# Summing a row-times-matrix product over 16 streamed weight blocks: on the tensor engine, or on the vector engine with a final sum over partitions

## The chip, the cores and the metric

The kernel runs on one core of a Trainium2 chip. The metric is the device time of one execution in microseconds (us). PE is the tensor engine (matmuls; PEld is its weight load), DVE the vector engine, ACT the scalar engine, POOL the GpSimd engine, SP the engine that issues most DMAs. Each engine works through its own instructions in the order in which the program gives them, and waits on semaphores for what others produce.

## What is computed

Two transformer blocks over 256 tokens of width 1024. The first block begins with a modulation: six rows of 1024 numbers, made from one conditioning vector `c`.

```python
sc = jax.nn.silu(c)
shift1, scale1, gate1, shift2, scale2, gate2 = jnp.split(sc @ w_mod + b_mod, 6, axis=-1)
h = modulate(rms_norm(x, norm1_g), shift1, scale1)
y, _ = token_mixer(h, hc, P, last)       # attention, gated linear attention (gla), hyena; merged by w_out
x = x + gate1[:, None, :] * y
h = modulate(rms_norm(x, norm2_g), shift2, scale2)
x = x + gate2[:, None, :] * grouped_moe(h, ...)
```

The change concerns the last four of the six rows (gate1, shift2, scale2, gate2), "the second modulation": a vector of 1024 times a matrix of 1024 x 4096, 16 MB of float32. The rows are first used where `w_out`'s result is evicted, so there is the whole token mixer to stream the matrix in.

## The kernel before

**Tiling.** `stream_order` (L249) lays all weights out as blocks of mostly 1 MB (128 partitions x 8 KB). `load` (L501) has SP fetch them in that order into buffers of the tag u8, of which there are 19 of 8 KB per partition (`BUFS`, L325); weight pieces, activations and other large tiles use the same 19. An ordinary weight piece is split by `stream` (L527) into a rounded high part (ACT) and the rest (DVE), and `feat_block` (L624) multiplies it: one half block is 24 matmuls of 256 columns. The second modulation's matrix comes as 16 blocks of [128, 2048] (`mod2`): blocks 0 to 7 are the eight chunks of the contraction for the first 2048 columns (the first half: gate1, shift2), blocks 8 to 15 for the other 2048 (scale2, gate2). They stand between the blocks of the three branches, by `MOD2_BRG` and `MOD2_BR` (L334): 0 to 3 beside the gate columns `w_brg` of the attention branch, 4 to 7 beside `w_br_att`, 8 to 11 beside `w_brg` of gla, 12 and 13 beside `w_br_gla`, 14 and 15 beside the first two blocks of `w_brg` of hyena.

**The product.** `mod_block` (L1353) multiplies one block when its place comes. `mod_rows` (L815) issues four matmuls, one for each 512 columns; the weights on the array are a column of `cs` (silu of `c`) padded to 32 columns, so the four results stand in partition groups 0, 32, 64 and 96 of one PSUM bank, held over eight blocks. After block 7 and after block 15 DVE adds the bias tile `bm` to it; `mod_spread` (L1389) then splits the sum into high and low part and copies each row to all 128 partitions by matmuls with `pick`, a matrix with ones in rows 0, 32, 64 and 96. `mod_spread` is a generator: for the first half one step of it is taken at the start of each of blocks 8 to 15, for the second half all steps are taken by `spread` (L1502) ahead of the last quarter of `w_out`.

**The order of the work around it.** The program is emitted in one sequence, and each engine keeps that order. Main work (weight blocks) is emitted in order; the chains of attention, gla and hyena are generators whose steps are put between the main work by a planner, `Side` (L383) with `Clocked` (L341). The planner keeps a clock for PE, ACT and DVE of its own: a matmul of n columns costs n/2400 us (4n/2400 if its operands are not rounded ones or n is under 256), a DVE operation 0.07 + n/960, an ACT operation 0.06 + n/1150. After each piece of main work `tick` looks whether a step is due:

```python
def tick(self):
    if self.jobs and Clocked.now["P"] >= self.next()[1]:
        self.step()
# step: wait = next(job); if wait: due = Clocked.now["P"] + wait
#       else: due = (last end of an ACT or DVE operation of the step) + 0.15
def finish(self, g):          # emits what is left of job g, step after step
    while any(j[0] is g for j in self.jobs):
        self.step(...)
```

Three lines of the main program call `finish` (L1428): attention must be complete before `w_br_att` starts, gla before `w_br_gla`, hyena before `w_br_hy`. Only one step goes at a tick. Attention's steps ask for a wait of 6.0; most of gla's and hyena's are due 0.15 after their last ACT or DVE operation. Between 160 and 455 us of the trace this sets the order. The `w_out` product follows (`lin_sq`, L1453, call at L1560), then the router and the experts.

Of the kernel before, what the change touches and what calls it, by code (L numbers as in the profile page):

```python
# [12 lines left out]
AF = mybir.ActivationFunctionType  # L13
OP = mybir.AluOpType
# [4 lines left out]
D = 1024  # L19
# [363 lines left out]
class Side:  # L383
# [10 lines left out]
    def next(self):  # L394

        a = self.jobs[:2]
        return a[1] if len(a) > 1 and a[1][2] is a[0][0] and a[1][1] < a[0][1] else a[0]
# [22 lines left out]
def program(ctx, tc, A, out, dump=None):  # L420
# [5 lines left out]
    V, S, G, P = nc.vector, nc.scalar, nc.gpsimd, nc.tensor  # L426
    V, S, P = Clocked(V, "V"), Clocked(S, "S"), Clocked(P, "P")
# [4 lines left out]
    def T(shape, name, dt=F32, tag=None):  # L432
        n = 4
        for s in shape[1:]:
            n *= s
        if tag is None:
            for t, lim in (("us", 128), ("uh", 512), ("u1", 1024), ("u2", 2048), ("u4", 4096), ("u8", 8192)):
                if n <= lim:
                    tag = t
                    break  # L440
        uid[0] += 1
        t = sb.tile(list(shape), dt, tag=tag, bufs=BUFS.get(tag, 1), name=f"{name}{uid[0]}")
        return t

    def T2(shape, name):

        n = 4 * math.prod(shape[1:])
        if n > 4096:
            return T(shape, name + "H", F32R), T(shape, name + "L", F32R)
        t = T([shape[0], 2, *shape[1:]], name, F32R)  # L450
        return t[:, 0], t[:, 1]

    def PS(name="ps"):
        uid[0] += 1
        t = pp.tile([128, 512], F32, tag="ps", bufs=8, name=f"{name}{uid[0]}")
        return t

    def mm3(ps, aH, aL, bH, bL, start, stop):
        P.matmul(ps, aH, bH, start=start, stop=False)
        P.matmul(ps, aH, bL, start=False, stop=False)  # L460
        P.matmul(ps, aL, bH, start=False, stop=stop)

    def split(h, l, src):
        S.activation(h, src, AF.Copy)
        V.tensor_tensor(l, src, h, op=OP.subtract)
# [86 lines left out]
    def take(name, b, u=0):  # L552
        i, v = pieces[pos["take"]]
        assert order[i][:2] == (name, b) and u == v, (order[i], v, name, b, u)
        stream()
        pos["take"] += 1
        return halves.pop((i, u)) if order[i][4] is not None else raws.pop(i)
# [66 lines left out]
    def feat_block(name, b, x, per=1):  # L624

        for u in range(2):
            wh, wl = take(name, b, u)
            for j in range(per):
                g = u * per + j
                if g % 2 == 0:  # L630
                    ps = PS()
                lin_feat(wh, wl, j, x, ps[:, (g % 2) * 256:(g % 2) * 256 + 256])
                side.tick()
                if g % 2:
                    yield ps
# [10 lines left out]
    def C(name):  # L646
        g, sl = CCOLS[name]
        return cg[g][:, sl]
# [21 lines left out]
    rows = {}  # L670
# [13 lines left out]
    pick = T([128, 128], "pick", F32R)  # L684
# [7 lines left out]
    st = {}  # L692
# [119 lines left out]
    cs = T([128, 8, 32], "cs", tag="cs")  # L812
    V.memset(cs, 0.0)

    def mod_rows(w, k, ps):  # L815
        for j in range(4):
            P.matmul(ps[32 * j:32 * j + 32], cs[:, k], w[:, 0, j * 512:j * 512 + 512], start=k == 0, stop=k == 7)
# [46 lines left out]
    mrow = T([128, 512], "mrow")  # L864
# [41 lines left out]
    def by_k(pair):  # L906
        return lambda k: (pair[0][:, k], pair[1][:, k])

    def xs_of(pair):
        def f(k, m):  # L910
            c = slice(m * 128, m * 128 + 128)
            return pair[0][:, k, c], pair[1][:, k, c]
        return f
# [158 lines left out]
    ps = PS()  # L1072
# [275 lines left out]
    hyj = side.add(hyj)  # L1348


    acc2, mod2, spreads = {}, [], []

    def mod_block(i):  # L1353

        hf, k = divmod(i, 8)
        w = take("mod2", i)
        if hf:
            next(spreads[0], None)
        if k == 0:
            acc2[hf] = PS("mod")  # L1360
        mod_rows(w, k, acc2[hf])
        if k == 4:
            st["bm"] = bm = T([128, 512], "bm", tag="u4")
            V.memset(bm, 0.0)
            for j in range(4):
                S.dma_start(bm[32 * j:32 * j + 1], A["b_mod2"][:, hf * 2048 + j * 512:hf * 2048 + j * 512 + 512])
        if k == 7:
            bm = st["bm"]
            V.tensor_tensor(bm, acc2.pop(hf), bm, op=OP.add)
            spreads.append(mod_spread(st.pop("bm")))  # L1370
            if False:
                next(spreads[hf])

    rw = Pc("router_w").rearrange("p (k e) -> p k e", k=8)

    def turned_half(src, k4):
        pt = PS()
        for k in range(4):
            P.transpose(pt[:, k * 128:k * 128 + 128], src[:, (4 * k4 + k) * 128:(4 * k4 + k) * 128 + 128], ident)
        t = T([128, 512], "h2T")  # L1380
        S.activation(t, pt, AF.Copy)
        return t

    def logits(ts, ps, start, stop):

        for k in range(8):
            P.matmul(ps, ts[k // 4][:, k % 4 * 128:k % 4 * 128 + 128], rw[:, k], start=start and k == 0, stop=stop and k == 7)

    def mod_spread(rows):  # L1389

        rH, rL = T2([128, 512], "mrow")
        split(rH, rL, rows)
        yield
        for a in range(2):
            t = T([128, D], "mod2")
            for n in range(2):
                ps = PS()
                q = slice(32 * (2 * a + n), 32 * (2 * a + n) + 32)
                P.matmul(ps, pick[q], rH[q], start=True, stop=False)
                P.matmul(ps, pick[q], rL[q], start=False, stop=True)  # L1400
                S.activation(t[:, n * 512:n * 512 + 512], ps, AF.Copy)
            mod2.append(t)
        yield
        if len(mod2) == 2:
            ts = [turned_half(mod2[1], k4) for k4 in range(2)]
            yield
            ps = PS()
            logits(ts, ps[:, :16], True, True)
            st["shifted"] = T([128, 16], "shifted", tag="uh")
            V.tensor_copy(st["shifted"], ps[:, :16])  # L1410

    msum = mH = mL = None
    n_mod = 0
    for b, br in ((2, "att"), (1, "gla"), (0, "hy")):
        g = T([128, 8, 256], "gate")
        for j in range(4):
            ps, = feat_block("w_brg", 4 * b + j, by_k(hs[0]))
# [13 lines left out]
        if br == "hy":  # L1431
            xt = T([128, 2, D], "x")
            G.dma_start(xt, A["x"].rearrange("(m p) d -> p m d", p=128))
            mH, mL = T2([128, 8, 256], "m")
        per = 2 if br == "att" else 4
        for i in range(8 // per):
            for j, ps in enumerate(feat_block("w_br_" + br, i, ys, per // 2)):
                c = slice(per * i + 2 * j, per * i + 2 * j + 2)
# [10 lines left out]
        if br == "att":  # L1449
            msum = g  # L1450
    dump("mH", mH)

    def lin_sq(name, xs, evac, before=(), quarters=(0, 1, 2, 3), whole=None):  # L1453


        ps = {(m, n): PS() for m in range(2) for n in range(2)}
        kept = []

        def go(m, n, q, w):
            for k in range(2):  # L1460
                first, last = q == quarters[0] and k == 0, q == quarters[3] and k == 1
                if whole and q in WHOLE:
                    P.matmul(ps[m, n], whole(2 * q + k, m), w[:, k, n * 512:n * 512 + 512], start=first, stop=last)
                else:
                    h, l = xs(2 * q + k, m)
                    mm3(ps[m, n], h, l, w[0][:, k], w[1][:, k], first, last)
            side.tick()

        for i, q in enumerate(quarters):
            if q in before:  # L1470
                before[q]()
            if i == 2 and "prepare" in st:
                st.pop("prepare")()
            for n in range(2):
                if n == 0 or not (whole and q in WHOLE):
                    block = take(name, q, n)
                w = (n, q, block)
                go(0, *w)
                if i:
                    kept.append(w)  # L1480
                else:
                    go(1, *w)
                if i == 3:
                    evac(0, n, ps[0, n])
        for n in range(2):
            for w in kept:
                if w[0] == n:
                    go(1, *w)
            evac(1, n, ps[1, n])
# [67 lines left out]
        P.matmul(pa[m][n], ident, x1[:, m, n * 512:n * 512 + 512], start=True, stop=False)  # L1557

    psr = PS()
    lin_sq("w_out", xs_of((mH, mL)), ev_out, {3: spread}, whole=lambda k, m: msum[:, k, m * 128:m * 128 + 128])  # L1560
    for k4 in range(2):
        turned.append(turned_half(h2s[1][0], k4))
        if not k4:
# [25 lines left out]
    def ahead(v, count):  # L1589
# [21 lines left out]
                           op0=OP.is_lt, op1=OP.mult)  # L1611
# [4 lines left out]
    ps = PS()  # L1616
# [80 lines left out]
    with tc.If(full > CAP, label="full"):  # L1697
# [10 lines left out]
        for e in range(N_EXP):  # L1708
# [9 lines left out]
            for k in range(8):  # L1718
                for q in range(2):
                    w = fetch("gu", 8 * e + k, q)  # L1720
                    for m in range(2):
                        P.matmul(gu[q, m], fT[m][:, k * 128:k * 128 + 128], w, start=k == 0, stop=k == 7)
            for m in range(2):
                hf, ht, ps = hfs[m], hts[m], gu[0, m]
# [6 lines left out]
            for k in range(4):  # L1731
                for n in range(2):
                    w = fetch("down", 4 * e + k, n)
# [83 lines left out]
    for w, n in (("a", 8), ("b", 16)):  # L1817
# [4 lines left out]
        k = T([128, 2 * n], "rk", tag="us")  # L1822
# [26 lines left out]
    for e in range(N_EXP):  # L1849
# [3 lines left out]
        ps = PS()  # L1853
# [504 lines left out]
```

## Time and profile before

| | |
|---|---|
| median of 3 runs | 1425.87 us (1422.07 to 1426.35) |
| the profiled execution | 1420.13 us, of it a span of 1418.4 us from the first to the last instruction |
| PE, PEld busy | 96%, 75% of the span |
| DVE, ACT busy | 59%, 45% |
| mean granted clock of PE | 0.992 of 2.4 GHz |

An operation's duration in the profile overlaps with the next one's start on the same engine, so where many follow each other the distance of their starts is the price. A matmul in plain float32 shows as two records.

### The profile page before, as it was taken

The page shows a single profiled execution, that of the slowest core. Times are in us where ns is not written, and L with a number is a line of the kernel's source. Part 1 is how long each engine was busy: PE and PEld are TensorE (multiplying, and loading weights), DVE is VectorE, ACT ScalarE, POOL GpSimd, SP SyncE. Part 2 cuts the span into 40 slices and gives each one's busy share as a digit, 9 for nine tenths or more (in the row PEclk, how much of TensorE's full clock was granted, in tenths as well). Part 3 has the DMA queues.
Part 4 walks back from the last instruction along what each step waited for, and adds up shares of the span by engine and source line. Part 5 has one row for each costly group of instructions (what it writes and reads, how often), then busy time and mean ns, then how long its engine had stood idle before and what let it go on. Part 6 is the DMA issues. An engine that isn't in the chain of part 4 may idle for free.

```text
span 1418.4 us, 20472 instructions
## 1 busy us (share of the span) xinstructions
PE 1365.9 (96%) x8334; PEld 1065.1 (75%) x8334; DVE 836.1 (59%) x1519; ACT 634.6 (45%) x1020; POOL 5.8 (0%) x13
## 2 busy tenths in 40 slices
PE   6999999999999899999999899999999998999998
PEld 2678899878797444343488679999978887999996
DVE  5777457446766511211465586666676888566675
ACT  5544465544333311111357555544526673455541
POOL 0000000000000000000000000000000000000000
PEclk9999999999999999999999999999999999999999
DMA  9523344635469799999742345555444353555630
GB/s 373 219 71 119 149 151 154 247 130 196 161 210 360 307 421 420 421 420 421 275 179 89 119 145 182 208 178 208 165 162 149 127 179 135 191 179 178 215 142 30
DMA packets 44481, 297.42 MB, mean 210 GB/s; under 512 B 5170, under 2 KB 6370, under 8 KB 10016
## 3 DMA queue, kind: packets, MB, share of 16 engines
q1 hardware_dynamic: 41868, 291.02, 54.6%
q10 hardware_dynamic: 1924, 3.27, 0.7%
q0 software_dynamic: 592, 1.79, 0.5%
q8 instruction: 67, 1.10, 0.3%
q14 instruction: 30, 0.25, 0.0%
HBM read 295.00 MB, written 1.05 MB: 209 GB/s over the span
## 4 chain that ended last, share of the span: by engine, by line
PE 56%; DVE 5%; ACT 2%; DMA 1%; issue 1%; ACTq 0%; SPq 0%; DVEq 0%
PE ps L379 47%; PE pd L379 7%; DVE w L379 2%; PE pa L379 1%; PE pq L379 1%; ACT pe L379 1%; DVE v L379 1%; DMA raw<-in_ab_q 1%; DVE sm L379 1%; ACT w L379 0%; DVE rs L379 0%; PE oc L379 0%; DVE xL L379 0%; DVE rsa L379 0%; DMA pt<-in_p 0%
## 5 line engine op out<-in xcount | busy, mean ns | idle before, releaser
L379 DVE TENSOR_TENSOR w<-raw,w 128x1024 fp32r<-128x1024 f32 (+3 forms) x301 | 346.4, 1194 | 84.5 <-ACT w L379 83.4
L379 ACT ACTIVATE w<-raw 128x1024 fp32r<-128x1024 f32 (+3 forms) x301 | 293.5, 1033 | 10.8 <-DVE w L379 4.8
L379 PE MATMUL ps<-xH,w 128*128 128x256 f32 x1408 | 256.5, 283 | 0.6 <-ACT xH L379 0.6
L379 PEld LDWEIGHTS ps<-xH,w 128*128 128x128 f32 x1408 | 220.6, 192 | 1.8 <-ACT xH L379 1.1
L379 PE MATMUL ps<-xL,w 128*128 128x256 f32 x704 | 199.3, 283 | 0.7 <-DVE xL L379 0.7
L379 PE MATMUL ps<-w,xH 128*128 128x512 f32 (+2 forms) x544 | 150.3, 362 | 4.0 <-ACT xH L379 2.1
L379 PEld LDWEIGHTS ps<-xL,w 128*128 128x128 f32 x704 | 134.9, 192 | 1.8 <-DVE xL L379 1.1
L379 PE MATMUL pd<-w,fh 128*128 128x512 f32 x528 | 125.6, 394 | 0.0
L379 PE MATMUL ps<-raw,xg 128*64 128x512 f32 x512 | 121.3, 605 | 3.3 <-DVE posf L379 3.3
L379 PE MATMUL ps<-hH,w 128*128 128x256 f32 (+1 forms) x608 | 115.7, 287 | 0.0
L379 PEld LDWEIGHTS pd<-w,fh 128*128 128x128 f32 x528 | 98.2, 188 | 21.6
L379 PEld LDWEIGHTS ps<-w,xH 128*128 128x128 f32 x544 | 95.3, 189 | 19.4 <-ACT xH L379 4.0
L379 PEld LDWEIGHTS ps<-hH,w 128*128 128x128 f32 (+1 forms) x608 | 94.9, 187 | 7.9 <-issue 2.7
L379 PE MATMUL ps<-w,xL 128*128 128x512 f32 (+2 forms) x272 | 97.7, 359 | 1.9 <-DVE xL L379 1.7
L379 PE MATMUL ps<-w,hH 128*128 128x512 f32 (+1 forms) x288 | 88.1, 389 | 0.0
L379 PE MATMUL ps<-hL,w 128*128 128x256 f32 (+1 forms) x304 | 85.9, 282 | 0.0
L379 PEld LDWEIGHTS ps<-raw,xg 128*64 128x64 f32 x512 | 34.0, 138 | 59.7 <-issue 57.6
L379 DVE SCALAR_TENSOR_TENSOR fc<-ps,par,fc 128x255 f32<-128x255 f32 x88 | 42.4, 482 | 51.6 <-ACT fc L379 50.0
L379 ACT ACTIVATE fc<-ps,par 128x256 f32<-128x256 f32 x44 | 24.8, 564 | 92.3 <-PE ps L379 66.4
L379 PEld LDWEIGHTS ps<-w,hH 128*128 128x128 f32 x288 | 52.1, 188 | 13.8 <-issue 2.7
L379 PEld LDWEIGHTS ps<-w,xL 128*128 128x128 f32 x272 | 51.2, 188 | 11.9 <-DVE xL L379 5.0
L379 PEld LDWEIGHTS ps<-hL,w 128*128 128x128 f32 (+1 forms) x304 | 56.9, 187 | 0.6
(444 smaller groups left out, 1853.5 us busy)
## 6 DMA issues: line engine op xcount, KB each, us to landing
raw<-in_moe_gu SPq DMA_DIRECT2D x63, 1024.0 KB, 12.9
raw<-in_moe_down SPq DMA_DIRECT2D x32, 1024.0 KB, 11.3
raw<-in_mod SPq DMA_DIRECT2D x24, 1024.0 KB, 4.9
raw<-in_ffn_gate SPq DMA_DIRECT2D x22, 1024.0 KB, 4.8
raw<-in_ffn_up SPq DMA_DIRECT2D x22, 1024.0 KB, 4.9
raw<-in_ffn_down SPq DMA_DIRECT2D x22, 1024.0 KB, 4.8
raw<-in_w_brg SPq DMA_DIRECT2D x12, 1024.0 KB, 5.6
raw<-in_ple_gate SPq DMA_DIRECT2D x8, 1024.0 KB, 4.7
```

The costliest lines, as they stand in the source:

```text
L379: return f(*args, **kw)
```

## The change

The 16 blocks are no longer multiplied on PE. For each block DVE multiplies the block by the chunk of `cs` (one number per partition) and adds it to an accumulator `acc` of [128, 2048] in SBUF, in two operations of 1024 columns. `acc` takes one of the 19 buffers. At block 0 and block 8 POOL clears a new `acc` and then, on its own DMA queue, loads the bias into partition 0 (before, four DMAs of ACT's queue did that into `bm`, at blocks 4 and 12). After blocks 7 and 15 `mod_spread` splits `acc` in two parts of 1024 columns, and sums the 128 partitions with a matrix of ones (made once in the tile of `pick`), which at the same time puts the sum on all partitions. It has more steps than before (split, matmuls, split, matmuls); the second half's first split is emitted ahead of the third quarter of `w_out`, the rest ahead of the fourth.

```diff
--- before.py
+++ after.py
@@ -1348,7 +1348,9 @@
     hyj = side.add(hyj)
 
 
-    acc2, mod2, spreads = {}, [], []
+    mod2, spreads = [], []
+    ones = pick
+    S.activation(ones, C("ones16"), AF.Copy, scale=16.0)
 
     def mod_block(i):
 
@@ -1357,19 +1359,15 @@
         if hf:
             next(spreads[0], None)
         if k == 0:
-            acc2[hf] = PS("mod")
-        mod_rows(w, k, acc2[hf])
-        if k == 4:
-            st["bm"] = bm = T([128, 512], "bm", tag="u4")
-            V.memset(bm, 0.0)
-            for j in range(4):
-                S.dma_start(bm[32 * j:32 * j + 1], A["b_mod2"][:, hf * 2048 + j * 512:hf * 2048 + j * 512 + 512])
+            st["acc"] = acc = T([128, 2048], "acc")
+            G.memset(acc, 0.0)
+            G.dma_start(acc[0:1], A["b_mod2"][:, hf * 2048:hf * 2048 + 2048])
+        acc = st["acc"]
+        for n in range(2):
+            c = slice(n * 1024, n * 1024 + 1024)
+            V.scalar_tensor_tensor(acc[:, c], w[:, 0, c], cs[:, k, 0:1], acc[:, c], op0=OP.mult, op1=OP.add)
         if k == 7:
-            bm = st["bm"]
-            V.tensor_tensor(bm, acc2.pop(hf), bm, op=OP.add)
-            spreads.append(mod_spread(st.pop("bm")))
-            if False:
-                next(spreads[hf])
+            spreads.append(mod_spread(st.pop("acc")))
 
     rw = Pc("router_w").rearrange("p (k e) -> p k e", k=8)
 
@@ -1386,21 +1384,20 @@
         for k in range(8):
             P.matmul(ps, ts[k // 4][:, k % 4 * 128:k % 4 * 128 + 128], rw[:, k], start=start and k == 0, stop=stop and k == 7)
 
-    def mod_spread(rows):
-
-        rH, rL = T2([128, 512], "mrow")
-        split(rH, rL, rows)
-        yield
+    def mod_spread(acc):
+
         for a in range(2):
+            rH, rL = T2([128, D], "mrow")
+            split(rH, rL, acc[:, a * D:a * D + D])
+            yield
             t = T([128, D], "mod2")
             for n in range(2):
                 ps = PS()
-                q = slice(32 * (2 * a + n), 32 * (2 * a + n) + 32)
-                P.matmul(ps, pick[q], rH[q], start=True, stop=False)
-                P.matmul(ps, pick[q], rL[q], start=False, stop=True)
+                for r in (rH, rL):
+                    P.matmul(ps, ones, r[:, n * 512:n * 512 + 512], start=r is rH, stop=r is rL)
                 S.activation(t[:, n * 512:n * 512 + 512], ps, AF.Copy)
             mod2.append(t)
-        yield
+            yield
         if len(mod2) == 2:
             ts = [turned_half(mod2[1], k4) for k4 in range(2)]
             yield
@@ -1557,7 +1554,7 @@
         P.matmul(pa[m][n], ident, x1[:, m, n * 512:n * 512 + 512], start=True, stop=False)
 
     psr = PS()
-    lin_sq("w_out", xs_of((mH, mL)), ev_out, {3: spread}, whole=lambda k, m: msum[:, k, m * 128:m * 128 + 128])
+    lin_sq("w_out", xs_of((mH, mL)), ev_out, {2: lambda: next(spreads[1]), 3: spread}, whole=lambda k, m: msum[:, k, m * 128:m * 128 + 128])
     for k4 in range(2):
         turned.append(turned_half(h2s[1][0], k4))
         if not k4:
```

## Rows read from the trace of the kernel before

**Rows 1.** The page, part 1: busy us of each engine, share, instructions.
```profile
PE 1365.9 (96%) x8334; PEld 1065.1 (75%) x8334; DVE 836.1 (59%) x1519; ACT 634.6 (45%) x1020; POOL 5.8 (0%) x13
```

**Rows 2.** Stretches: length, busy PE, PEld, DVE, ACT, POOL, PE clock, DMA share, GB/s.
```profile
150.00:200.00 50.00, 50.00 (x372) 43.95 (x371) 24.86 (x47) 25.08 (x45) 0.00 (x0) 1.00 0.45 169
...
345.00:375.00 30.00, 27.63 (x204) 23.90 (x206) 22.35 (x39) 11.55 (x14) 0.00 (x0) 0.94 0.46 172
375.00:405.00 30.00, 29.24 (x194) 24.08 (x190) 25.14 (x36) 10.94 (x16) 0.00 (x0) 1.00 0.50 176
```

**Rows 3.** Timeline (start us, us, what), PE around block 2, and block 15.
```profile
185.77 0.28 PE L379 MATMUL ps<-hL,w 128*128 128x256 f32 x1
185.89 0.28 PE L379 MATMUL ps<-hH,w 128*128 128x256 f32 x1
186.10 1.06 PE L379 MATMUL mod<-raw,cs 128*32 128x512 f32 x8
187.10 0.38 PE L379 MATMUL ps<-hH,w 128*128 128x256 f32 x1
...
400.77 1.06 PE L379 MATMUL mod<-raw,cs 128*32 128x512 f32 x8
```

**Rows 4.** Tile mod: DVE's scale-and-add of 1024 columns (min/median/max ns); timeline: three 1024-column DVE operations.
```profile
L379 DVE SCALAR_TENSOR_TENSOR mod<-mod,g2n x1: 1225/1225/1225, 447.0 to 447.0; 128x1024 f32<-128x1024 f32 x1
...
349.36 3.49 DVE L379 TENSOR_TENSOR w<-raw,w 128x1024 fp32r<-128x1024 f32 x3
```

**Rows 5.** Timeline: the end of gla, normalised, turned and split.
```profile
339.49 1.07 ACT L379 ACTIVATE osq<-o 128x512 f32<-128x512 f32 x2
...
340.76 0.68 DVE L379 TENSOR_REDUCE ov<-osq 128x4 f32<-128x512 f32 x1
...
348.75 0.69 DVE L379 TENSOR_TENSOR oy<-oy,gog 128x512 f32<-128x512 f32 x1
...
349.05 1.32 PE L379 MATMUL ps<-c_base,oy 128*128 128x128 f32 x8
...
349.97 0.60 ACT L379 ACTIVATE yg<-ps 128x512 fp32r<-128x512 f32 x1 [5.08 <-PE ps L379]
```

**Rows 6.** Timeline, DVE: hyena's last two frequency blocks and its result.
```profile
396.65 0.69 DVE L379 TENSOR_TENSOR ya<-ps,spec 128x512 f32<-128x512 f32 x1 [1.52 <-PE ps L379]
...
403.31 0.68 DVE L379 TENSOR_TENSOR YL<-yc,YH 128x512 fp32r<-128x512 f32 x1
...
407.36 0.68 DVE L379 TENSOR_TENSOR ya<-ps,spec 128x512 f32<-128x512 f32 x1
...
411.99 0.69 DVE L379 TENSOR_TENSOR YL<-yc,YH 128x512 fp32r<-128x512 f32 x1
...
416.32 0.69 DVE L379 TENSOR_TENSOR yt<-ps,uc 128x512 f32<-128x512 f32 x1 [0.73 <-PE ps L379]
```

**Rows 7.** Timeline: the second half's spread, and a rounded matmul beside it.
```profile
442.99 0.62 PE L379 MATMUL ps<-w,mH 128*128 128x512 f32 x2
...
445.12 0.75 PE L379 MATMUL ps<-mrow,pick 32*128 32x512 f32 x8
445.81 5.42 PE L379 MATMUL ps<-raw,gate 128*128 128x512 f32 x12
...
445.89 2.06 ACT L379 ACTIVATE mod<-ps 128x512 f32<-128x512 f32 x4 [8.00 <-PE ps L379]
```

**Rows 8.** Stretches of 2 us in hyena, columns as in rows 2.
```profile
365.00:367.00 2.00, 0.68 (x3) 0.19 (x1) 2.00 (x2) 2.00 (x4) 0.00 (x0) 1.00 0.00 0
367.00:369.00 2.00, 1.14 (x3) 0.95 (x4) 1.40 (x3) 0.70 (x2) 0.00 (x0) 0.62 0.00 0
369.00:371.00 2.00, 2.00 (x7) 1.57 (x6) 0.60 (x1) 0.00 (x0) 0.00 (x0) 0.53 0.00 0
```

**Rows 9.** A POOL clear of 1024 columns; a small DMA of POOL's queue (KB, us to landing).
```profile
28.80 0.94 POOL L748 MEMSET filt<- 1x1024 f32 x1 [25.46 <-DVE filt L379]
...
row_r<-in_row_r POOLq DMA_DIRECT2D x1, 8.0 KB, 5.3
```

## The prediction

> **What bounds the kernel now.** I began with the busy times. PE stands at 96% and DVE at 59% [rows 1], which says that PE is the engine to relieve, but it is an average. The second modulation lies between 160 and 405 us, so I cut that part into stretches [rows 2]. PE is busy without a gap in the first of them; from 345 to 405 it is idle for 2.4 + 0.8 us, and there DVE has 22.4 and 25.1 us of 30. So in this part the time is PE's queue, and the side chains of attention, gla and hyena cost nothing, because the planner has put main matmuls beside nearly every step of them. The question is therefore double: what leaves PE's queue, and whether that cover stays.
>
> **What leaves PE.** One block is eight records, busy 1.06 us together: the four matmuls run beside each other in the four column groups. Ordinary matmuls around it start every 0.12 us, the one before the block at 185.89, the one after it at 187.10, so the block takes 1.21 - 0.12 = 1.09 us [rows 3]. With 1.07 for each of the 16 blocks (all look alike in the trace) PE loses **17.1 us**. Nothing waits for a block's result before the spread.
>
> **What DVE gets.** 32 operations of 1024 columns. The same operation on such a tile took 1.225 us; in a row such operations follow each other every 1.13 us [rows 4]. That is 36 to 39 us, and 3 us more for the larger splits less what `bm` cost. Spread over the 245 us that is 16% more. In the three stretches read DVE has 72 of 110 us, 66% [rows 2], so as an engine over the whole it does not become the bound. But the last block stands at 400.77 [rows 3], and 13 and 14 ahead of it in the same stretch, where DVE has 25.1 of 30 us already; 3 x 2.3 = 6.9 more makes 32.0, over the 30 that there are. There the chains will be late by some us; I count that at hyena's end, below.
>
> **What happens to the order.** The planner prices a block at 4 x 4 x 512/2400 = 3.41 us of PE, over three times what the trace shows, and puts steps by its PE clock. After the change it prices it at nothing on PE and at 2.27 on DVE's clock. I use its formulas for the order alone, never for a time.
> Attention: a step costs 4.69 on the planner's PE clock and the next is due 6.0 later, so 10.69 after the last one's start. A half block is 2.56. Before: step, half, block of the modulation (10.66, just too early), half: one step every two halves. After: step and three halves (12.37). The first branch has 8 halves of `w_brg` and 12 of `w_hyu`: steps went at halves 1, 3, 5, 7, 9, 12, 15, 18, and now at 1, 4, 7, 10, 13, 16, 19. One more step is left for `finish`, transposes and products whose inputs are long there: 0 to 1.5 us, I take 0.
> Gla: before, its last step went one tick ahead of the last one before `finish`. Between `w_br_att` and that point the planner's PE clock loses eight blocks, 27 of 117, and the dues that hang on DVE's clock move later. Walking the ticks through by the formulas, four steps are left for `finish`: two of matmuls on the accumulators, the normalisation, and turning and splitting its result.
> Hyena: before, its last step went at the third tick from the end. Now two are left: the second frequency block's products, and the inverse transform.
> What is left at a `finish` has no main matmul beside it, and PE, in order, waits.
>
> **The prices of the two joins, from rows of the same work.** Gla: DVE's part runs from 340.76 to 349.44, 8.7 us; ahead of it the square on ACT (0.6 and a hand-over of 0.3), behind it transposes, of which 0.9 is PE's own, and the split: ACT 0.6 after them, then DVE about 0.6 [rows 5]. PE idle about 10 us; 5 if two of the four steps still find a place, 13 if DVE has block 11's two operations in front. I take **10**.
> Hyena: the first frequency block keeps DVE from 396.65 to 404.0 (7.3), the second from 407.36 to 412.7 (5.3) [rows 6]. Beside these 12.6 and one weight split of 1.2 PE has one half block (24 x 0.12 = 2.9), the second block's 12 matmuls (12 x 0.23 = 2.8) and half of the first's (1.4), so it waits 13.8 - 7.1 = 6.7; the result then passes DVE, ACT, DVE (416.32 to the next hand-over, about 2) before `w_br_hy` can begin. I take **8.5**, with bounds 4 and 12.
> Of the 3.1 us of waits that are there now [rows 2], 2.2 lie at hyena's first transform [rows 8] and stay; about **-1.5** goes or is counted in the joins, bounds -3 and -1.
>
> **The spread.** The eight matmuls of 32 rows run four beside each other, 445.12 to 445.81, 0.69 us; a full matmul of 512 columns takes 0.23 (0.62 less 0.39 for one more) [rows 7]. Eight of them in the first half: 1.84, so +1.15. In the second half the second split stands behind the first two copies on ACT: copies begin 0.77 after the matmuls and take 0.5 each (2.06 for four) [rows 7], so they end at 1.8; the high part (1.04) ends at 2.9, the rest on DVE (1.2) at 4.1, and PE is through at 5.0 instead of 0.7: +4.3. Behind these matmuls, in PE's queue, stands the last quarter of `w_out`, which nothing else holds. Sum **+5.4**, bounds 3.5 and 6.5.
>
> **The clock.** In hyena PE is idle 1.3 and 0.9 us in two stretches of 2 us, and the granted clock of the stretches behind them is 0.62 and 0.53: part and nearly all at 1.2 instead of 2.4 GHz. That lost 0.38 x 2 + 0.47 x 2 = 1.7 us [rows 8]. Each of the two new joins is a longer idle stretch than those; I take 1.7 for each, **+3.4**, bounds 0 and 5.1.
>
> **What is new on queues.** POOL clears 2048 columns (two of the kind that took 0.94) and then moves 8 KB (a DMA of that queue landed after 5.3 us) [rows 9]: some 7 us from the moment the buffer is free to the first addition, at blocks 0 and 8. Queued behind the waiting DVE are weight splits, and PE has some four half blocks split ahead. The buffer is the one that has been free longest, and nothing else stands in POOL's queue until 411 us. I take 0, bounds 0 and 4 us. One or two of the 19 buffers fewer: loads and splits find a free one later; 0 to 4. The bias DMAs leave ACT's queue: nothing, since ACT is free there.
>
> **The sum.** -17.1 - 1.5 + 10 + 8.5 + 5.4 + 3.4 = **+8.7 us**. The profiled execution took 1420.13 (span 1418.4), which gives 1428.8; it lies 5.7 under the median of the three runs, to which I add it: 1434.6, **1434.5 us**.
>
> **Rivals.** (a) *The saving arrives whole*: if the planner's order keeps each step covered, only the spread is to be paid: -17.1 - 1.5 + 5.4 = -13, 1413 us. For it speaks that DVE is free on average. The Trainium skill, page "Perfetto Trace Analysis", section "Identifying Performance Opportunities", says it as a rule: improve the most-contended engine. By that rule, too, the time falls. Against (a): before, gla and hyena were just done at their joins, so nothing of the cover was spare. 0.12.
> (b) *It cancels*: both joins cost half (5 and 4.5), and the clock recovers at once: -17.1 - 1.5 + 9.5 + 5.4 = -3.7, 1422; with one of the two at full price +1. 0.21.
> (c) *DVE becomes the bound from 345 on*, by the 32.0 us that it is to do in 30, or the accumulator's buffer holds splits back: another 8 to 12 on the forecast, 1445. It decides where weight splits wait for DVE. 0.12.
> (d) The forecast, 1428 to 1442 by the joins' bounds: 0.55.
>
> **Range and chances.** About 0.3%, 4.3 us, is what a measurement of this kernel can tell from no change. Faster by more: (a) and a little of (b), 0.14. Within: most of (b) and the lowest part of the forecast, 0.23. Slower: 0.63. Range 1421 to 1446: it leaves out most of (a) and the upper part of (c).
>
> **What would show it.** PE: no `mod<-raw` records from 160 on; a wait on `oy` of 5 to 10 us ahead of the transposes at gla's end, a wait on `YH` of some 7 us in hyena's last inverse transform, with granted clocks near 0.5 behind both; a wait of 2 us and one of 1 us among the spread's matmuls in `w_out`. DVE: 32 operations writing `acc`, 1.2 us each. If PE is busy through both joins, the reading of the order was wrong, and (a) holds; if PE waits on `w` in many places, (c).

## The result and the profile after

The kernel with the change takes **1447.3 us** (median of 4 runs, 1445.3 to 1450.4), the kernel before 1426.1 us: a ratio of 1.0146, interval 1.0116 to 1.0177. The change costs 21 us. The prediction was 1434.5 us, range 1421 to 1446: the direction was right, the size was not, and the time lies 1.3 us above the range.

The profiled execution of after took 1450.4 us (span 1448.6), that of before 1420.1, some 30 us apart. Of these, 5.5 us lie ahead of the change: PE's order is the same up to the first matmul of `w_brg`, which starts at 150.69 us before and at 156.18 after, and the granted clock of the stretch from 20 to 40 us is 0.93 before and 0.68 after. Another 3.8 us come behind the first matmul of the experts, which the change doesn't touch. From the first matmul of `w_brg` to the first of the experts it is 330.09 us before and 350.97 after, **+20.9 us**, close to the 21.2 by which the medians differ. That stage is taken apart below.

The page of after, part 1: busy us of each engine.

```profile
PE 1367.2 (94%) x8206; PEld 1075.4 (74%) x8206; DVE 875.5 (60%) x1549; ACT 640.5 (44%) x1024; POOL 10.4 (1%) x17
```

The 16 blocks are gone from PE, yet its busy time is as in [rows 1]: part of its work ran at the lower clock. DVE has 39 us more. The stretches of after, columns as in [rows 2]:

```profile
150.00:200.00 50.00, 50.00 (x369) 47.34 (x368) 32.74 (x53) 26.77 (x45) 2.31 (x2) 1.00 0.48 174
345.00:375.00 30.00, 18.51 (x126) 16.98 (x127) 22.48 (x46) 11.61 (x17) 0.00 (x0) 0.77 0.31 105
375.00:405.00 30.00, 25.38 (x182) 23.96 (x181) 22.99 (x30) 8.36 (x11) 0.00 (x0) 0.94 0.45 165
405.00:430.00 25.00, 19.29 (x109) 16.45 (x108) 20.30 (x28) 10.26 (x13) 2.90 (x5) 0.90 0.61 208
...
450.00:475.00 25.00, 22.57 (x79) 14.61 (x78) 12.68 (x17) 8.15 (x13) 0.00 (x0) 0.93 0.93 371
```

In the first stretch PE is as full as before. From 345 to 405 us it stands idle for 11.5 and 4.6 us, where before had 2.4 and 0.8, and then for 5.7 and 2.4 more; the granted clock of these four is 0.77, 0.94, 0.90 and 0.93. The waits themselves, from PE's timeline of after (start us, us, what, and in brackets the idle time ahead and what ended it); these are all of 0.5 us or more up to the router, then the one ahead of the experts:

```profile
248.06 1.99 PE L379 MATMUL ps<-pT,kv 128*128 128x256 f32 x8 [1.17 <-ACT pT L379]
312.80 0.71 PE L379 MATMUL ps<-qkT 64*128 64x128 f32 x8 [1.73 <-ACT qkT L379]
337.80 1.13 PE L379 MATMUL ps<-gv,ke 64*128 64x256 f32 x4 [0.78 <-ACT gate L379]
352.05 0.66 PE L379 MATMUL ps<-c_base,oy 128*128 128x128 f32 x2 [8.27 <-DVE oy L379]
356.25 1.54 PE L379 MATMUL ps<-c_base,oy 128*128 128x128 f32 x6 [3.54 <-DVE oy L379]
373.02 2.32 PE L379 MATMUL ps<-z,fwd 128*128 128x512 f32 x9 [0.76 <-DVE z L379]
394.57 0.50 PE L379 MATMUL ps<-hH,w 128*128 128x256 f32 x2 [0.76 <-DVE w L379]
400.51 0.38 PE L379 MATMUL ps<-hH,w 128*128 128x256 f32 x1 [3.05 <-ACT w L379]
401.77 0.80 PE L379 MATMUL ps<-hH,w 128*128 128x256 f32 x2 [0.76 <-DVE w L379]
424.66 0.50 PE L379 MATMUL ps<-inv,YH 128*128 128x256 f32 x2 [2.03 <-ACT YH L379]
429.42 0.79 PE L379 MATMUL ps<-inv,YH 128*128 128x256 f32 x2 [3.46 <-ACT YH L379]
439.48 0.38 PE L379 MATMUL ps<-yh,w 128*128 128x256 f32 x1 [0.73 <-ACT yh L379]
465.34 0.49 PE L379 MATMUL ps<-mrow,pick 128*128 128x512 f32 x1 [1.67 <-ACT mrow L379]
466.60 1.65 PE L379 MATMUL ps<-mrow,pick 128*128 128x512 f32 x3 [0.77 <-DVE mrow L379]
...
507.15 8.31 PE L379 MATMUL ps<-raw,xg 128*64 128x512 f32 x30 [5.83 <-DVEq L1694]
```

They are 29.5 us up to the router, against 2.9 before (1.11, 1.07 and 0.76, in hyena). Gla's end costs 11.8, hyena's 5.5 + 0.7, the spread 2.4, as the forecast had it in kind. The three waits for `w` at 394 to 402 us (4.6) and those for `qkT` and `gate` (2.5) are what it had priced at nothing. From the router (the wait for `mask`) to the experts it takes 14.5 us instead of 11.0.

Ahead of the wait for `qkT` DVE stood still. Timelines of after, POOL's and DVE's, at block 8:

```profile
292.97 1.80 POOL L1363 MEMSET acc<- 128x2048 f32 x1 [125.63 <-PE ps L379]
...
298.24 2.48 DVE L379 SCALAR_TENSOR_TENSOR acc<-raw,cs,acc 128x1024 f32<-128x1024 f32 x2 [6.07 <-issue]
```

The second accumulator's buffer came free only at 292.97, when PE had done with it. Then POOL cleared it and loaded the bias, and DVE, next in whose queue stood block 8's addition, waited 6.1 us, with weight splits and the steps that lead to `qkT` behind it. The profile names no releaser for this wait ("issue"); the bias's DMA, issued at 295.06 us, fits: the slower of the two took 3.1 us to land.

Behind the waits for `w` stands SP's queue. Timelines of SP before, then of SP and ACT after:

```profile
355.20 0.33 SPq L515 DMA_DIRECT2D raw<-in_w_brg  x1
375.99 0.33 SPq L515 DMA_DIRECT2D raw<-in_mod  x1
...
362.26 0.33 SPq L515 DMA_DIRECT2D raw<-in_w_brg  x1
384.80 0.33 SPq L515 DMA_DIRECT2D raw<-in_mod  x1
385.18 5.60 SPq L515 DMA_DIRECT2D raw<-in_w_brg  x2
...
392.20 1.06 ACT L379 ACTIVATE w<-raw 128x1024 fp32r<-128x1024 f32 x1 [9.22 <-DMA raw<-in_w_brg]
```

SP issued no load for 22 us, because the load next in its queue (a block of the modulation) had no free buffer, the one thing that a load waits for here; the `w_brg` blocks stood behind it, and ACT then waited 9.2 us for one of them to land. The gap by itself is not new: before, SP stood 20.5 us ahead of such a block too, and ACT waited for no load.

The additions themselves, from the view of tile acc (min/median/max ns), were little dearer than the 1225 ns of [rows 4]; POOL's clear of 2048 columns took what [rows 9] gives for two of 1024 (1.80 us, above):

```profile
L379 DVE SCALAR_TENSOR_TENSOR acc<-raw,cs,acc x32: 1272/1279/1285, 172.6 to 407.5; 128x1024 f32<-128x1024 f32 x32
```

### The profile page after: what moved, and what is told of

Its sections match the earlier page's. It is cut to its first block, busy times and chain, and to the rows that moved or that the text cites. A ratio compares the mean times of both kernels' runs of the same rounds, so it can differ in the third digit from the quotient of the medians.

```text
span 1448.6 us, 20255 instructions
## 1 busy us (share of the span) xinstructions
PE 1367.2 (94%) x8206; PEld 1075.4 (74%) x8206; DVE 875.5 (60%) x1549; ACT 640.5 (44%) x1024; POOL 10.4 (1%) x17
## 4 chain that ended last, share of the span: by engine, by line
PE 55%; DVE 5%; ACT 2%; DMA 1%; issue 1%; ACTq 0%; SPq 0%; DVEq 0%
PE ps L379 46%; PE pd L379 7%; DVE w L379 2%; PE pa L379 1%; PE pq L379 1%; ACT pe L379 1%; DVE v L379 1%; DMA raw<-in_ab_q 1%; DVE sm L379 1%; ACT w L379 0%; DVE rs L379 0%; PE oc L379 0%; DVE xL L379 0%; DVE rsa L379 0%; DMA pt<-in_p 0%
## 5 line engine op out<-in xcount | busy, mean ns | idle before, releaser
L379 PE MATMUL ps<-raw,xg 128*64 128x512 f32 x512 | 121.6, 607 | 5.8 <-DVEq L1694 5.8
## 6 DMA issues: line engine op xcount, KB each, us to landing
raw<-in_moe_gu SPq DMA_DIRECT2D x63, 1024.0 KB, 10.1
```

Source lines behind the costliest of these rows:

```text
L379: return f(*args, **kw)
```

## The experiments

The theory that stood behind the forecast is called **order**: the planner, told that a block costs nothing on PE and 2.3 us on DVE, leaves more steps to the joins. Its rivals are **DVE** (the additions delay the chains whatever the order), **buffers** (accumulator and split rows take buffers of 8 KB, which are held for long or come free late) and **spread**. All ratios are to the kernel before, 1426.1 to 1426.3 us.

**order_kept: the change, with the steps where they were.**

```
+            st["acc"] = [T([128, 1024], "acc") for _ in range(2)]
...
-            V.scalar_tensor_tensor(acc[:, c], w[:, 0, c], ...)
+            nc.vector.scalar_tensor_tensor(acc, w[:, 0, n * 1024:n * 1024 + 1024], ...)
+            Clocked.now["P"] += 2 * 512 / 600
...
```

> The changed kernel, but the planner's PE clock is advanced by 3.41 us for each block and the 32 additions are left out of its DVE clock, so that the side steps stand where they stood before the change; the accumulator lies in two tiles of 1024 columns in the buffers of 4 KB, because with this order the 19 buffers of 8 KB do not suffice. Theory 'order' (the loss is cover lost at the joins of gla and hyena): PE waits under 1 us for oy at gla's end and about 2 us in hyena as before, 17 us of PE work are saved and the spread costs 4 to 5: 1411 to 1418 us. Theory 'DVE' (its 41 us of additions delay the chains whatever the order): waits of 5 us or more stay at the joins, 1430 to 1445 us.

Measured: 1438.1 us, ratio 1.0074 (1.0047 to 1.0101). The wait for `oy` is gone, so the order made that one, and the kernel is 9 us faster than after. Not all of the 9 is the order's: the accumulator lies in buffers of 4 KB here too, and against acc_small below, which has these buffers and after's order, 4 us are left. But it is 12 us slower than before, inside the range of "DVE", where "order" wanted it 8 to 15 us faster. At gla's end PE now waits for something else (its timeline, then DVE's):

```profile
348.41 1.65 PE L379 MATMUL ps<-mrow,pick 128*128 128x512 f32 x3 [5.52 <-DVE mrow L379]
...
344.87 2.35 DVE L379 TENSOR_TENSOR w<-raw,w 128x1024 fp32r<-128x1024 f32 x2
347.14 1.22 DVE L379 TENSOR_TENSOR mrow<-acc,mrow 128x1024 fp32r<-128x1024 f32 x1
```

PE also waits 4.0 us for `att` and 4.1 for `yg`. The second split of the first half's accumulator stands in DVE's queue behind gla's normalisation and two weight splits, and PE has its matmuls next.

**order_alone: the kernel before, with the steps where the change puts them.** PE computes the blocks; the planner's clocks are set as if DVE did. DVE has no additions.

```
+        kept = Clocked.now["P"]
         mod_rows(w, k, acc2[hf])
+        Clocked.now["P"] = kept
+        for n in range(2):
+            Clocked.now["V"] += 0.07 + 1024 / 960 + 0.13 * n
...
```

> The kernel before, computing on PE as before, but the planner is told what it is told after the change (a block costs nothing on its PE clock and two additions on its DVE clock, the spread's splits have the prices and the places of the changed kernel): the side steps stand exactly where the changed kernel has them, and DVE has no additions. Theory 'order': the waits for oy (12 us in the changed kernel), YH (5.5) and their half clock come back, less what two or three blocks of 1.1 us fill: 1441 to 1452 us. Theory 'DVE' or 'buffers': with neither additions nor a held buffer the time stays within 4 us of the kernel before, 1422 to 1430 us.

Measured: 1445.6 us, ratio 1.0128 (1.0059 to 1.0197): +19.5 us, and +19.9 in the stage of the profiled executions. "Order" holds. PE's timeline has the same waits, with no addition on DVE:

```profile
362.87 0.66 PE L379 MATMUL ps<-c_base,oy 128*128 128x128 f32 x2 [7.53 <-DVE oy L379]
367.07 1.54 PE L379 MATMUL ps<-c_base,oy 128*128 128x128 f32 x6 [3.54 <-DVE oy L379]
...
433.61 0.50 PE L379 MATMUL ps<-inv,YH 128*128 128x256 f32 x2 [2.03 <-ACT YH L379]
438.38 0.80 PE L379 MATMUL ps<-inv,YH 128*128 128x256 f32 x2 [3.66 <-ACT YH L379]
...
400.21 1.06 ACT L379 ACTIVATE w<-raw 128x1024 fp32r<-128x1024 f32 x1 [5.17 <-DMA raw<-in_w_brg]
```

Of after's 11.8 us for `oy` the order alone makes 11.1, and of its 5.5 for `YH` all. The last row is ACT's: with this order ACT waits 5.2 us for a block of `w_brg`, though no accumulator and no wide split rows hold a buffer; PE doesn't wait for it here.

**acc_small: the change, with the accumulator in buffers of 4 KB.** The order is after's exactly.

```
-            st["acc"] = acc = T([128, 2048], "acc")
+            st["acc"] = [T([128, 1024], "acc") for _ in range(2)]
...
```

> The changed kernel with the order of its steps kept exactly; only the accumulator moves from one buffer of 8 KB to two of 4 KB, so that 19 buffers of 8 KB are there for loads and splits again. Theory 'buffers': the three waits for w in hyena (0.8 + 3.0 + 0.8 us), the late loads of raw and their half clock go away, 5 to 7 us: 1440 to 1443 us. Theory 'order' alone, with the waits for w due to DVE's additions: within 2 us of the changed kernel, 1445 to 1449 us.

Measured: 1442.2 us, ratio 1.0109 (1.0055 to 1.0163), 5.1 us under after by the medians, as "buffers" has it; the intervals of the two ratios overlap. In the profiled executions it is 4.0 us from the first matmul of `w_brg` to the router. The timelines of PE and ACT at the same place:

```profile
391.09 0.39 PE L379 MATMUL ps<-hH,w 128*128 128x256 f32 x1 [1.86 <-ACT w L379]
392.35 0.78 PE L379 MATMUL ps<-hH,w 128*128 128x256 f32 x2 [0.76 <-DVE w L379]
...
382.78 1.06 ACT L379 ACTIVATE w<-raw 128x1024 fp32r<-128x1024 f32 x1 [7.04 <-DMA raw<-in_w_brg]
```

The waits for `w` fall from 4.6 to 2.6 us. They don't vanish as expected: `w_brg` still comes late. The waits for `qkT` and `gate` in gla (2.5) are gone: POOL clears the second accumulator from 270.81 us on, and DVE no longer stands at block 8. So the run takes away two things, a buffer that is held and an accumulator that is late, and its 5.1 us are the price of both.

**dve_alone: the kernel before, with 32 additions of no use on DVE.**

```
         mod_rows(w, k, acc2[hf])
...
+        for n in range(2):
+            nc.vector.scalar_tensor_tensor(acc, w[:, 0, n * 1024:n * 1024 + 1024], cs[:, k, 0:1], acc, ...)
```

> The kernel before with its PE work and its order kept; 32 additions of 1024 columns like those of the change are put on DVE beside it, into a tile of 4 KB that nobody reads. Theory 'DVE' (41 us more on DVE delay the splits of weights and the side chains): 1434 to 1446 us, with waits for w and at the joins on PE. Theory 'order' (DVE has room as long as the steps are covered): 1425 to 1430 us.

Measured: 1443.2 us, ratio 1.0112 (1.0058 to 1.0166): +17.0 us, with PE's work and order untouched. This is what "order" alone can't give. The mechanism shows at 300 us, DVE's timeline before:

```profile
299.60 0.76 DVE L379 COPY_PREDICATED att<-mk,ps 128x256 f32<-128x256 int32 x2
```

and in dve_alone (DVE's, then PE's):

```profile
299.80 2.60 DVE L1367 SCALAR_TENSOR_TENSOR acc<-raw,cs,acc 128x1024 f32<-128x1024 f32 x2
302.31 0.76 DVE L379 COPY_PREDICATED att<-mk,ps 128x256 f32<-128x256 int32 x2
...
302.80 1.64 PE L379 MATMUL ps<-gv,ke 64*128 64x256 f32 x3 [3.04 <-DVE att L379]
361.94 8.29 PE L379 MATMUL ps<-yg,w 128*128 128x256 f32 x47 [2.64 <-DVE yg L379]
379.70 0.49 PE L379 MATMUL ps<-z,fwd 128*128 128x512 f32 x1 [3.68 <-ACT z L379]
```

DVE works its queue in order, and the 2.6 us of one block stand ahead of `att`, on which PE's next matmul waits. The waits of 0.5 us or more sum to 14.0 us instead of 2.9, and behind three of them the granted clock is 0.5 (303 to 309, 361 to 367 and 381.5 to 384 us), where the kernel before has one such place up to the router [rows 8].

**dve_half: the same additions, half as wide** (512 of each 1024 columns).

> As dve_alone (the kernel before with its PE work and order, and 32 additions of no use on DVE), but each addition has 512 columns instead of 1024, 0.7 us by the 512-column operations of the trace instead of 1.3; count, places and held buffers stay. Theory 'DVE time': the loss of dve_alone, 17 us, falls to about half or less, 1430 to 1435 us. Theory 'held buffers' or 'count of operations': the loss stays, 1440 to 1444 us.

Measured: 1434.5 us, ratio 1.0064 (1.0039 to 1.0088): +8.2 us, half of dve_alone's 17.0. The price goes by DVE's time, not by the number of operations or by the buffers held. (What the additions read and write is halved with their time; no run parts these two, but in the rows above it is the place in DVE's queue that makes `att` late.)

**spread_kept: order_kept, and both splits ahead of the spread's matmuls.** The edit is shown against order_kept.

```
+        rows = [T2([128, D], "mrow") for _ in range(2)]
         for a in range(2):
-            rH, rL = T2([128, D], "mrow")
-            split(rH, rL, acc[a])
-            yield
+            split(*rows[a], acc[a])
+        yield
+        for a in range(2):
...
```

> As order_kept, and both splits of a half's accumulator are issued before the first of the spread's matmuls, as the kernel before does with its one split: PE's order is then that of the kernel before exactly, less the 16 blocks. In order_kept PE waited 5.5 us for the first half's second split and 2.4 us for the second half's. Theory 'DVE' (what is left of the loss is the 32 additions in DVE's queue): these two waits and about 2 us of half clock go, the waits for att, yg, z, YH and YL (14 us in order_kept) stay: 1426 to 1431 us. Theory 'spread' (the spread's form is the larger part): the chains catch up too, 1411 to 1420 us.

Measured: 1427.5 us (ten runs, 1425.3 to 1436.7), ratio 1.0019 (0.999 to 1.0048). The waits for `mrow` are gone and 10.6 us with them; the rest stays, as "DVE" has it. The order is that of before, no accumulator is late and no split holds PE up; PE has 17 us of blocks less to do and some 2 us of spread more, and the time is that of before: the additions eat the saving. The split rows still hold two buffers of 8 KB; both_fp32, below, does without them and isn't faster.

**on_pool: the additions on POOL.** The edit is shown against spread_kept.

```
-            nc.vector.scalar_tensor_tensor(acc, w[...], cs[:, k, 0:1], acc, ...)
+            part = w[:, 0, n * 1024:n * 1024 + 1024]
+            G.tensor_scalar(part, part, cs[:, k, 0:1], None, op0=OP.mult)
+            G.tensor_tensor(acc, acc, part, op=OP.add)
```

> As spread_kept, but the additions are made by POOL (a product in place and an addition, 64 operations of 1024 columns) instead of DVE; PE's order, the buffers and the traffic stay. Theory 'DVE queue' (a chain's next step stands behind 2.6 us of additions): the waits for att, yg, z, YH and YL go back to the 3 us of the kernel before, 1409 to 1415 us. Theory 'held buffers and traffic' (the blocks' buffers are held longer and more is read and written beside the other engines): no gain over spread_kept, 1426 us or more. If POOL is too slow for 16 blocks in 245 us, loads are held back and PE waits for w: over 1440 us.

Measured: 1449.1 us, ratio 1.0162 (1.0122 to 1.0201). It is slower for a reason that none of its theories has: PE waits for the chains as before (6.3 us for `att`, 7.0 for `oy`, 4.4 for `z`), not for `w`, though DVE has no additions. Its longest wait, 8.9 us for `kn`, lies ahead of `w_brg`: POOL, with nothing else in its queue, begins the first block at 121.6 us, where DVE began it at 172.6 in after. So the places of the additions aren't kept either. PE's timeline there, then timelines at gla's end, POOL's and DVE's:

```profile
146.34 1.33 PE L379 MATMUL ps<-c_base,kn 128*128 128x128 f32 x5 [8.85 <-DVE kn L379]
...
356.66 2.37 POOL L1369 TENSOR_TENSOR acc<-acc,raw 128x1024 f32<-128x1024 f32 x1
359.01 2.83 POOL L1368 TENSOR_SCALAR raw<-raw,cs 128x1024 f32<-128x1024 f32 x1
...
356.84 2.21 DVE L379 TENSOR_TENSOR rsa<-rs 128x4 f32<-128x4 f32 x1
...
360.36 0.16 DVE L379 TENSOR_TENSOR rsa<-rs 128x4 f32<-128x4 f32 x1
```

The same DVE operation of 4 columns takes 0.16 us at 360.36 and 2.21 at 356.84, where it ends with POOL's addition (359.05 and 359.03). The Trainium skill, page "SBUF — State Buffer", section "Terms", has a pair of ports that DVE and POOL arbitrate for, held for the whole instruction while the other one blocks; this row agrees. The row at 360.36 doesn't: it lies beside POOL's product (359.01 to 361.84) and passes at its usual 0.16 us. So the additions delay the chains from POOL's queue too, and whether DVE's queue or what is held and moved beside it makes the loss, this run can't say.

**first_half and second_half: one half on DVE, the other on PE**, at before's order. The edit is first_half's; second_half has `(1,)` in place of `(0,)`.

```
+        if hf in (0,):
...
+                nc.vector.scalar_tensor_tensor(acc, w[:, 0, n * 1024:n * 1024 + 1024], ...)
...
+            return
         mod_rows(w, k, acc2[hf])
...
```

> The kernel before, with the first half's 8 blocks added up on DVE (two tiles of 4 KB) and spread as in spread_kept, and the second half's 8 blocks left on PE; PE's order is that of the kernel before. In dve_alone PE ran level with the kernel before up to 297 us and fell back from there on, where the second half's blocks are. Theory 'place' (an addition costs only where a chain ends on DVE): PE loses 8.6 us of work, the first half's additions cost nothing, its spread 1 to 4 us: 1418 to 1422 us. Theory 'amount' (the price goes by the additions, 17 us for 32): 1426 - 8.6 + 8.5 + 1 to 3: 1426 to 1429 us.

> The mirror of first_half: the first half's blocks stay on PE, the second half's 8 are added up on DVE. Theory 'place': 1426 - 8.6 + 17 and about 1 for the spread: 1433 to 1437 us, with the waits of dve_alone at yg, z, YH and YL. Theory 'amount': 1426 to 1429 us.

Measured: first_half 1421.3 us (ratio 0.9953, 0.9926 to 0.9979). In these two and in first_half_fp32 the half left on PE was spread with ones over all 32 rows of a group, so its two vectors were other ones; second_half sent the tokens another way through the experts, took 2463 us and can't be compared. Both were made again with the picked row:

> first_half again with the half that stays on PE spread by the picked row, as the kernel before does (in first_half ones took all 32 rows of a group, so that this half's four vectors were others). The instructions on the path are the same: theory 'place' 1418 to 1422 us, theory 'amount' 1426 to 1429 us.

> second_half again with the picked row in the first half (in second_half its vectors were others, and the tokens took another way through the experts). PE's order is that of the kernel before. Theory 'place': 1426 - 8.6 + 17 and about 1 for the spread: 1433 to 1437 us, with the waits of dve_alone at att, yg, z, YH and YL. Theory 'amount': 1426 to 1429 us.

Measured: first_only 1420.2 us, ratio 0.9968 (0.9947 to 0.9988); second_only 1436.2 us, ratio 1.0069 (1.0041 to 1.0097). "Place" holds on both sides. As many additions leave 6.0 of PE's 8.6 us in the first half, and in the second they take all of it and 10.1 more. dve_alone agrees: up to block 8 PE runs level with before, and all of its 17.0 us come behind that. PE's timeline of second_only has the waits again:

```profile
303.27 0.58 PE L379 MATMUL ps<-hH,w 128*128 128x256 f32 x1 [3.42 <-DVE att L379]
359.10 1.22 PE L379 MATMUL ps<-yg,w 128*128 128x256 f32 x4 [3.62 <-DVE yg L379]
```

**first_half_fp32, both_fp32, first_only_fp32: no splits in the spread.**

```
-                P.matmul(ps, ones, r[:, n * 512:n * 512 + 512], ...)
-                S.activation(t[:, n * 512:n * 512 + 512], ps, AF.Copy)
+                nc.tensor.matmul(ps, C("ones16"), rows[a][:, c], start=True, stop=True)
+                S.activation(t[:, c], ps, AF.Copy, scale=16.0)
...
```

> As first_half, but the spread multiplies the accumulator itself (float32) with ones/16 and ACT scales by 16, so that its two splits (2.1 us of ACT, 2.4 of DVE) and their two buffers go; PE has 4 matmuls of float32 in place of 8, by the price of the float32 rows about 2 us more. If the splits are what delays att behind the first half: 1 to 3 us faster than first_half. If not: 2 us slower.

> Both halves on DVE as in spread_kept, with the float32 spread of first_half_fp32 in both. Theory 'place': the second half's waits stay, 1423 to 1430 us; it does not come under first_half. If splits and their buffers were a large part of spread_kept's loss: 1413 to 1419 us.

> first_half_fp32 again with the picked row in the second half: 8 blocks on DVE where no chain ends on it, float32 spread without splits, order and places of the kernel before. Theory 'place': PE's 8.6 us less what the spread adds arrive nearly whole, 1416 to 1420 us, the fastest of all; theory 'amount': 1424 us or more.

Measured: first_half_fp32 1418.1 us (0.9951, 0.9926 to 0.9975); both_fp32 1432.6 us (1.0047, 1.0018 to 1.0077), a little above its expectation and not under spread_kept, so neither the splits nor their buffers were what that run lost; first_only_fp32 **1417.4 us** (0.9929, 0.9903 to 0.9956), faster than both kernels. Against first_only it is 2.8 us by the medians; the intervals overlap. Its waits on PE of 0.5 us or more are hyena's old three and no more (two of them here; 1.11, 1.07 and 0.79):

```profile
365.01 0.50 PE L379 MATMUL ps<-z,fwd 128*128 128x512 f32 x1 [1.11 <-ACT z L379]
...
386.27 0.50 PE L379 MATMUL ps<-YL,inv 128*128 128x512 f32 x1 [0.79 <-DVE YL L379]
```

From `w_brg` to the experts its profiled execution takes 322.0 us against 330.1: of the 8.6 us of the 8 blocks, 8.1 arrive.

## Why the prediction was wrong in size

The stage of the profiled executions, term by term:

| step of the prediction | predicted, us | measured, us | from |
|---|---|---|---|
| what leaves PE | -17.1 | -17.1, as priced | all 128 records of the blocks are gone from PE |
| waits that were there | -1.5 | -2.2 | 2.9 before, 0.8 after |
| gla's join | +10 (5 to 13) | +11.8 | 8.27 + 3.54 for `oy` |
| hyena's join | +8.5 (4 to 12) | +6.2 | 2.03 + 3.46 + 0.73 |
| the spread | +5.4 (3.5 to 6.5) | +4.7 | 2.4 of waits, 2.3 of work (16 x 0.23 - 2 x 0.69) |
| the clock | +3.4 (0 to 5.1) | +5.6 | a remainder: what is left of the stage up to the router |
| attention's join | 0 (0 to 1.5) | +1.2 | the wait for `pT` |
| one or two of 19 buffers fewer | 0 (0 to 4) | +4.6 | the three waits for `w`; 2.0 of it gone in acc_small |
| from the free buffer to the first addition | 0 (0 to 4) | +2.5 | `qkT`, `gate`; gone in acc_small |
| from the router to the experts | not in it | +3.5 | 14.5 against 11.0 |
| sum | +8.7 | +20.9 | |

**What held.** What leaves PE, the waiting places, the order of the steps and, within their bounds, the prices of both joins are right: order_alone gives their +19.5 without a single addition on DVE, against the 20.4 that the forecast had for joins, clock and the waits already there. PE is full through the first stretch and waits once, 1.2 us, up to 300 us.

**Which steps failed.** The largest is the paragraph "What is new on queues": two of its terms, taken at 0, cost PE 7.1 us of waits. "The buffer is the one that has been free longest" did not hold for the second accumulator: its buffer came free at 292.97 us, and DVE stood 6.1 us behind it (2.5 of PE's waits). "One or two of the 19 buffers fewer: loads and splits find a free one later" stands against the 4.6 for `w`. acc_small, which removes the accumulator's part of both, is 5.1 us faster by the medians, 4.0 in the stage. The other 2.6 of the waits for `w` stay there, and order_alone's 5.2 us of ACT speak for the order as the reason why `w_brg` is late; the forecast asked what the order does to the joins, not what it does to the loads. Rival (c) named a held buffer, with "PE waits on `w` in many places" as its sign; it stood beside the forecast, not in its sum.

The second step is the clock, 5.6 instead of 3.4. An estimate from PE's busy time and granted clock in stretches of 2 us gives 8.3 us lost after and 1.5 before: 2.3 and 3.2 behind the two joins, where the forecast took 1.7 each, and 2.9 behind the waits for `w` and `mrow`, which it did not count; the old loss in hyena is gone. (Its 1.7 for that one counts idle time too; over PE's busy time [rows 8] give 1.4.) The third is the 3.5 us behind the router, which the prediction didn't look at; about 1 of them is work at the lower clock, and 2.5 are discussed below.

**What the forecast left out and the sum hides.** "As an engine over the whole it does not become the bound" was true and of no use. dve_alone costs 17.0 us with the order of before: of its 41 us of additions the half behind block 8, where PE waits for the chains, is paid nearly in full, though DVE is busy 59% of the span [rows 1]. So rival (a), "if the planner's order keeps each step covered, only the spread is to be paid", fails at its condition: spread_kept has that cover and stands at 1427.5, not 1413. That the forecast, without a term for this, came as near as it did is luck: order and additions delay the same joins, and in after the two overlap: 19.5 and 17.0 alone, less 17.1, with 4.7 for the spread and 5 for buffers would be 29, and 21 is measured.

**The rule against it.** The Trainium skill, page "Perfetto Trace Analysis", section "Identifying Performance Opportunities", says to improve the most-contended engine. On the whole kernel the runs speak against it (1447.3); where only the blocks of the first half left PE, beside which the kernel before has no wait on PE, they agree (first_only_fp32, 1417.4).

**What stays open.** Why acc_small's `w_brg` still comes late isn't settled. order_alone, which has no accumulator, speaks for the order; but the splits of the spread still hold buffers of 8 KB in acc_small, and no run took those alone away at this order. Whether the 2.5 us ahead of the experts belong to the change isn't either.

## What to carry to other kernels

Work moved to an engine that is half idle is free only where no chain that the bounding engine waits for passes through that engine's queue; ask it stretch by stretch, and for what stands right behind the new operation. Where a planner places steps by its own prices, a change of a price moves the cover of every step behind it, so test the move of the work and the move of the order apart, each on the kernel before. And price the moment at which a new buffer comes free: an engine that works its queue in order waits for it, with everything that stands behind.

## What the hardware showed beside that

- POOL's additions stopped DVE: in on_pool one of DVE's operations of 0.16 us took 2.21 us and ended with POOL's addition, and the same operation beside the next product took 0.16 (rows of on_pool above). Groups by line and form (busy us, mean ns), POOL's two operations, and DVE's weight splits from 170 to 415 us, then in spread_kept from 165 to 410:

```profile
L1368 POOL TENSOR_SCALAR raw<-raw,cs 128x1024 f32<-128x1024 f32 x32 | 103.4, 3231 | 108.6 <-DMA raw<-in_mod 71.3 <-DVE sm L379 29.1 <-DVE ke L379 8.2
L1369 POOL TENSOR_TENSOR acc<-acc,raw 128x1024 f32<-128x1024 f32 x32 | 83.8, 2620 | 3.0 <-DMA acc<-in_b_mod 0.5
...
L379 DVE TENSOR_TENSOR w<-raw,w 128x1024 fp32r<-128x1024 f32 x46 | 67.5, 1486 | 26.0 <-ACT w L379 26.0
...
L379 DVE TENSOR_TENSOR w<-raw,w 128x1024 fp32r<-128x1024 f32 x46 | 55.7, 1223 | 25.7 <-ACT w L379 25.7
```

  POOL needs 5.9 us for what DVE does in one operation of 1.28.
- A spread of float32 with one matmul in place of two rounded ones, and no splits, cost PE nothing that the trace shows as a wait.
- Ahead of the experts the program branches. In the profiled execution of after DVE's first operation behind the branch waited 3.6 us, in that of before 1.1; the profiles of order_kept, order_alone, acc_small, dve_alone and spread_kept have PE's wait there at 3.3 to 3.4 us as before, not at after's 5.8. The trace doesn't say why.
